# Branch A of a hybrid encoder step: weight differences on DVE, and the accumulator read ahead of the weight preparation

## The chip, the cores and the metric

The kernel runs on one core of one Trainium2 chip. A core has a matrix engine (PE, with its weight loads shown as PEld), a vector engine (DVE), an activation engine (ACT), a general engine (POOL) and a queue that starts transfers (SP). Each engine works through its own list of instructions in the order in which they stand there; an instruction that has to wait holds up everything behind it on its engine. The metric is device microseconds (us) of the whole kernel; less is better. Before the change it was 1235.42 us, the median of three runs (1234.3 to 1236.22).

## What is computed

One layer of a streaming encoder on 1024 prompt tokens and 32 sample tokens, width 1024. The part that matters here is the input projection and branch A:

```
h = rmsnorm(x);  z = h @ w_in                      # 1056 x 1024  times  1024 x 8192
qa, fa, va, ga, xb, gb, qc, gc, za, zb, zc = split(z)
f  = lb + (1-lb)*sigmoid(fa)                       # branch A: gated linear recurrence, 4 heads x 128
oa = hgrn2(silu(qa), log f, 1-f, va, state)        # chunks of 64 tokens, a 128 x 128 state per head
pa = (rmsnorm(oa) * silu(ga)) @ w_a_down
pb = (lru(conv(xb)) * silu(gb)) @ w_b_down         # branch B
pc = (attention(qc, memory) * silu(gc)) @ w_c_down # branch C
y  = x + (sigmoid(za)*pa + sigmoid(zb)*pb + sigmoid(zc)*pc) @ w_out
```

All of it is float32 in effect: each matrix product is made of three products of a high and a low part.

## The kernel before, in words

The input projection is 32 products, each of them 256 output columns by all tokens, computed with Strassen's scheme in seven steps in place of eight (`WIDE` for the first 19 products, `NARROW` for the other 13, from `A_FROM` on). The activations stand ready in seven forms (A11, A12, A22, S1 to S4, each as a high and a low half). The weights of a step are a 512 x 128 block of `w_in` (`wraw`), or a difference of blocks: T1 = B12-B11, T2 = B22-T1, T3 = B22-B12 and T4 = B21-T2. The profile names the first two `T` and the last two, which are written over a block, `wraw`. `hl` splits such a block into a high half (ACT, line 41, `whi`) and a low half (DVE, line 44, `wlo`).

One step (`slot`, L362) issues, in this order:

- the first 12 matmuls (`product`, L349); then one piece of every running chain of side work (`advance`), first the fast ones, then the others;
- the other 12 matmuls; again one piece of each chain; and then everything that a table holds for this step (`run_sched`, L293): the split of the weights used three steps later, the four differences of the next product at fixed steps (T1 at a product's step 2, counted from 0, T2 at step 3, T3 at 5, T4 one product later at 1), and the loads of the product after the next at step 6;
- at the end `post` (L305), which reads the step's accumulator out of PSUM.

In the NARROW order the accumulators are X, Y, X, V, Z, V, Z for steps 0 to 6, in two buffers of PSUM. X is copied after step 0 (ACT, L310) and after step 2 (ACT, `c11`); Y is read after step 1 (DVE, L314, `u<-Y`); V is read after step 3 (DVE, L314, `p<-V`) and after 5, Z after 4 and 6 (DVE, lines 172, 764 to 770 and 839 to 845). V in step 3 takes the buffer of Y, so it may start only when `u<-Y` has ended; Z in step 4 takes that of X.

The 13 NARROW products are, for each of four heads, `AHand1` (f and v), `AHand2` (q and g) and a pair of branch C (`Row`, `zh`), and one merge-gate pair at the end. Each head's side work hangs on them: the elementwise chains of L774 and L848, and `hgrn` (L867), the recurrence, which begins in step 4 of the C product and ends in step 3 of the next head's first one. One piece of it is a few small matmuls on PE (`pu`, `po`), then on DVE `qr` (L924), `R` (L908) and `attm` (L886), on ACT the state `S`, a sum of squares and `kt` (L888), and on POOL the inverse root `rsr` (lines 97 and 98). Every third piece PE transposes `qr` (`pot`, L933).

The differences of weights are made by `sub`, on the engine that `eng` names: DVE for the first 19 products, POOL for the other 13. They are 512-column subtractions, four for each product.

Of the kernel before, what the change touches and what calls it, by code (L numbers as in the profile page):

```python
# [32 lines left out]
def kernel(ctx: ExitStack, tc: tile.TileContext, I, O):  # L33
    nc = tc.nc
# [43 lines left out]
    def advance(lst):  # L78
        for g in list(lst):
            try:  # L80
                next(g)
            except StopIteration:
                lst.remove(g)
# [51 lines left out]
    def dbank(name):  # L135
        return psum["d"].tile([128, 2, 512], F32, tag="d", name=name)

    def rblock(name):
        return wp.tile([128, 4, 128], F32, tag="wr", bufs=W_RAW, name=name)

    def load_block(src, r0, c0):
        t = rblock("wraw")
        nc.sync.dma_start(t, src[r0:r0 + 512, c0:c0 + 128].rearrange("(k p) c -> p k c", p=128))
        return t
# [6 lines left out]
    def hl(x, eng=None):  # L151
        h = wp.tile([128, 4, 128], F32R, tag="wh", bufs=W_HL, name="whi")
        l = wp.tile([128, 4, 128], F32R, tag="wl", bufs=W_HL, name="wlo")
        split(h, l, x, eng)
        return h, l
# [51 lines left out]
    A_FROM = len(pairs)  # L207
# [12 lines left out]
    def order(p):  # L220
        return NARROW if p >= A_FROM else WIDE
# [7 lines left out]
    def at(s, fn):  # L229
        sched.setdefault(s, []).append(fn)  # L230
# [3 lines left out]
    def plan(p):  # L234
        c1, c2, _ = pairs[p]
        pre = p < NPRE
        b = pos[p, 1 if pre else 0]
        R = {}

        def loads():  # L240
            R["B11"] = load_block(w_in, 0, c1)
            R["B12"] = load_block(w_in, 0, c2)
            R["B22"] = load_block(w_in, 512, c2)
            R["B21"] = load_block(w_in, 512, c1)

        eng = nc.gpsimd if p >= A_FROM else nc.vector

        def sub(out, x, y):
            eng.tensor_tensor(out, x, y, op=OP.subtract)

        def t1():
            R["T1"] = rblock("T1")
            sub(R["T1"], R["B12"], R["B11"])

        def t2():
            R["T2"] = rblock("T2")
            sub(R["T2"], R["B22"], R["T1"])

        def t3():
            sub(R["B12"], R["B22"], R["B12"])  # L260

        def t4():
            sub(R["B21"], R["B21"], R["T2"])

        def prep(k, name):
            if (p, k) in pos:
                e = pos[p, k]

                def go():
                    wts[e] = hl(R[name])  # L270

                at(e - 3, go)

        def pl():
            plt[p] = T1("p1l")
            nc.sync.dma_start(plt[p][:, :HF], p1d[p])

        at(b - 8, loads)
        at(b - 5, t1)
        at(b - 4, t2)  # L280
        at(b - 2, t3)
        R_NAME = {"T3": "B12", "T4": "B21"}
        for k, (_, name, _) in enumerate(order(p)):
            if name == "T4":
                at(b - 1 if pre else b + 1, t4)
            prep(k, R_NAME.get(name, name))
        if pre:
            at(max(b - 4, -1), pl)

    for p in range(NP):  # L290
        plan(p)

    def run_sched(s):  # L293
        for fn in sched.pop(s, []):
            fn()

    def v2(t):
        return t[:, :HF].rearrange("p (a n) -> p a n", a=2)
# [6 lines left out]
    def post(p, k, h):  # L305
        v = cur[order(p)[k][2]][:, :, :QF]

        def copy(name):
            cur[name] = H(name)
            nc.scalar.activation(v2(cur[name]), v, AF.Copy)  # L310

        def plus(name, tag, x):
            y = H(tag)
            nc.vector.tensor_tensor(v2(y), v, v2(cur[x]), op=OP.add)  # L314
            cur[name] = y

        if p >= A_FROM:
            if k == 0:
                copy("p1")
            elif k == 1:  # L320
                plus("u2", "u2", "p1")
            elif k == 2:
                h.c11(v, None)
            elif k == 3:
                plus("u4", "p1", "u2")
            elif k == 4:
                h.c22(v, cur["u4"])
            elif k == 5:
                h.c12(v, cur["u2"])
            else:  # L330
                h.c21(v, cur["u2"])
            return
        pre = p < NPRE
        if k == 0:
            copy("p1")
        elif k == 1:
            plus("p5", "p5", "p1") if pre else copy("p5")
        elif k == 2:
            plus("u2", "u2", "p1") if pre else copy("u2")
        elif k == 3:  # L340
            h.c11(v, cur["p1"])
        elif k == 4:
            h.c22(v, cur["p5"])
        elif k == 5:
            h.c12(v, cur["u2"])
        else:
            h.c21(v, cur["p1"] if pre else None)

    def product(ps, w, name, new, after=lambda q: None):  # L349
        wh, wl = w  # L350
        fh, fl = FORM[name]
        kw = {} if new else {"skip_group_check": True}
        for q in range(2):
            qs = slice(q * QF, (q + 1) * QF)
            o = ps[:, q, :QF]
            for i in range(4):
                nc.tensor.matmul(o, wh[:, i, :], fh[:, i, qs], start=bool(new) and i == 0, stop=False, **kw)  # L357
                nc.tensor.matmul(o, wh[:, i, :], fl[:, i, qs], start=False, stop=False, **kw)  # L358
                nc.tensor.matmul(o, wl[:, i, :], fh[:, i, qs], start=False, stop=(i == 3), **kw)  # L359
            after(q)  # L360

    def slot(e):  # L362
        p, k = ex[e]
        if "h" not in cur or cur["h"][0] != p:
            cur["h"] = (p, pairs[p][2]())
            if p < NPRE:
                cur["p1"] = plt.pop(p)
        form_, _, name = order(p)[k]
        new = (p, name) not in opened
        if new:  # L370
            opened.add((p, name))
            cur[name] = dbank(name)

        def after(q):
            advance(fast)
            advance(chains)
            if q == 1:
                run_sched(e)

        product(cur[name], wts.pop(e), form_, new, after)  # L380
        post(p, k, cur["h"][1])


    fb = fstack.enter_context(tc.tile_pool(name="forms_b", bufs=1, reuse_waits="tile"))
# [132 lines left out]
    def T1(name, dt=F32):  # L517
        return cpool.tile([128, NT + 6], dt, tag="t", bufs=P_T, name=name)

    def H(name, bufs=1):  # L520
        return cpool.tile([128, HF], F32, tag=name, bufs=bufs, name=name)
# [497 lines left out]
    for e in range(NE):  # L1019
        if ex[e] == (A_FROM, 0):  # L1020
            open_psum(4, 2)
        slot(e)
# [459 lines left out]
```

## Time and profile before

| | |
|---|---|
| median of three runs | 1235.42 us (1234.3 to 1236.22) |
| profiled execution, its own time | 1238.35 us |
| its span | 1236.4 us |
| PE, PEld busy | 93%, 90% |
| DVE, ACT, POOL busy | 59%, 45%, 20% |
| differences of weights on DVE / on POOL | 76 / 52 instructions |
| mean TensorE clock granted | 0.967 of full speed |

Busy time is a share of the span. What a stage's limit is stands in the waits of that stage: the idle time of an engine before an instruction, and which instruction of which engine ended it. A matmul of the projection lasts 0.28 us but the next one starts 0.12 us after it, so PE is full when matmuls start 0.12 us apart.

### The profile page before, as it was taken

The page shows a single profiled execution, that of the slowest core. Times are in us where ns is not written, and L with a number is a line of the kernel's source. Part 1 is how long each engine was busy: PE and PEld are TensorE (multiplying, and loading weights), DVE is VectorE, ACT ScalarE, POOL GpSimd, SP SyncE. Part 2 cuts the span into 40 slices and gives each one's busy share as a digit, 9 for nine tenths or more (in the row PEclk, how much of TensorE's full clock was granted, in tenths as well). Part 3 has the DMA queues.
Part 4 walks back from the last instruction along what each step waited for, and adds up shares of the span by engine and source line. Part 5 has one row for each costly group of instructions (what it writes and reads, how often), then busy time and mean ns, then how long its engine had stood idle before and what let it go on. Part 6 is the DMA issues. An engine that isn't in the chain of part 4 may idle for free. (4 is left out here: it accounts for less than half of the span.)

```text
span 1236.4 us, 21526 instructions
## 1 busy us (share of the span) xinstructions
PE 1145.9 (93%) x8350; PEld 1109.9 (90%) x8350; DVE 734.4 (59%) x1332; ACT 562.2 (45%) x1131; POOL 243.9 (20%) x382
## 2 busy tenths in 40 slices
PE   5677899999999999999999999998799999999998
PEld 5667899999999999899898998997699989899997
DVE  4445456776686686675565565654545567687222
ACT  4433346666657657563354343633433343443111
POOL 3540000000000001232333323330000004364111
PEclk8878899999999999999999999998999989899999
DMA  6125313213213313221312203116745245591221
GB/s 206 54 80 166 110 49 105 90 59 100 94 59 95 98 64 104 79 73 52 86 44 65 80 33 105 36 64 234 245 136 168 83 146 172 183 314 49 103 90 39
DMA packets 141705, 130.11 MB, mean 105 GB/s; under 512 B 10904, under 2 KB 122180, under 8 KB 141604
## 3 DMA queue, kind: packets, MB, share of 16 engines
q1 hardware_dynamic: 141604, 128.75, 33.0%
q8 instruction: 65, 1.06, 0.4%
q14 instruction: 36, 0.29, 0.1%
HBM read 93.93 MB, written 34.79 MB: 104 GB/s over the span
## 5 line engine op out<-in xcount | busy, mean ns | idle before, releaser
L44 DVE TENSOR_TENSOR wlo<-wraw,whi 128x512 fp32r<-128x512 f32 x208 | 155.0, 750 | 132.3 <-ACT whi L41 131.0
L61 PE MATMUL psdn<-ph,whi 128*128 128x384 f32 (+1 forms) x384 | 128.3, 334 | 7.7 <-ACT ph L41 5.8
L41 ACT ACTIVATE whi<-wraw 128x512 fp32r<-128x512 f32 x208 | 126.3, 620 | 17.4 <-PE psmem L1005 6.7
L61 PE MATMUL psdn<-pl,whi 128*128 128x384 f32 (+1 forms) x384 | 126.4, 329 | 0.1
L61 PE MATMUL psdn<-ph,wlo 128*128 128x384 f32 (+1 forms) x384 | 126.2, 329 | 0.2 <-DVE wlo L44 0.2
L61 PEld LDWEIGHTS psdn<-ph,whi 128*128 128x128 f32 x384 | 74.1, 193 | 10.6 <-ACT ph L41 6.5
L357 PE MATMUL V<-S1h,whi 128*128 128x264 f32 x256 | 75.0, 293 | 8.3 <-DVE u L314 7.5
L357 PE MATMUL X<-A11h,whi 128*128 128x264 f32 x256 | 76.8, 300 | 4.1 <-ACT pv L463 2.6
L44 DVE TENSOR_TENSOR wlo<-T,whi 128x512 fp32r<-128x512 f32 x64 | 44.3, 692 | 58.2 <-ACT whi L41 58.2
L359 PE MATMUL X<-A11h,wlo 128*128 128x264 f32 x256 | 75.6, 295 | 0.0
L358 PE MATMUL X<-A11l,whi 128*128 128x264 f32 x256 | 75.5, 295 | 0.0
L61 PEld LDWEIGHTS psdn<-pl,whi 128*128 128x128 f32 x384 | 73.9, 192 | 1.0 <-DVE pl L44 0.7
L61 PEld LDWEIGHTS psdn<-ph,wlo 128*128 128x128 f32 x384 | 73.6, 192 | 0.9 <-DVE wlo L44 0.9
L357 PE MATMUL V<-S4h,whi 128*128 128x264 f32 x256 | 73.7, 288 | 0.0
L359 PE MATMUL V<-S1h,wlo 128*128 128x264 f32 x256 | 73.3, 286 | 0.0
L358 PE MATMUL V<-S1l,whi 128*128 128x264 f32 x256 | 73.1, 286 | 0.0
L359 PE MATMUL V<-S4h,wlo 128*128 128x264 f32 x256 | 72.8, 285 | 0.0
L358 PE MATMUL V<-S4l,whi 128*128 128x264 f32 x256 | 72.7, 284 | 0.0
L61 PE MATMUL psout<-woh,mhi 128*128 128x384 f32 (+3 forms) x216 | 68.9, 319 | 0.1
L61 PE MATMUL psout<-woh,mlo 128*128 128x384 f32 (+3 forms) x216 | 68.7, 318 | 0.2 <-DVE mlo L44 0.2
L61 PE MATMUL psout<-wol,mhi 128*128 128x384 f32 (+3 forms) x216 | 68.7, 318 | 0.0
L174 ACT ACTIVATE zh<-zh 128x528 f32<-128x528 f32 x36 | 23.3, 646 | 95.7 <-DVE zh L172 56.3
(365 smaller groups left out, 3819.9 us busy)
## 6 DMA issues: line engine op xcount, KB each, us to landing
wraw<-in_w_in SPq DMA_DIRECT2D x134, 256.0 KB, 3.5
pbd<-sgb SPq DMA_DIRECT2D x8, 528.0 KB, 2.6
zda<-zh SPq DMA_DIRECT2D x16, 264.0 KB, 2.6
zdc<-zh SPq DMA_DIRECT2D x16, 264.0 KB, 2.8
wraw<-in_w_b_down SPq DMA_DIRECT2D x16, 256.0 KB, 4.5
xf<-in_x_prompt SPq DMA_DIRECT2D x8, 512.0 KB, 3.9
wraw<-in_w_out SPq DMA_DIRECT2D x16, 256.0 KB, 4.4
out<-xf SPq DMA_DIRECT2D x8, 512.0 KB
```

What stands on the lines that cost most here:

```text
L41: nc.scalar.activation(out, in_, AF.Copy)
L44: (eng or nc.vector).tensor_tensor(out, a, hi.bitcast(F32), op=OP.subtract)
L61: nc.tensor.matmul(ps, a, b, start=st, stop=sp)
L174: nc.scalar.activation(t, t, self.act)
L357: nc.tensor.matmul(o, wh[:, i, :], fh[:, i, qs], start=bool(new) and i == 0, stop=False, **kw)
L358: nc.tensor.matmul(o, wh[:, i, :], fl[:, i, qs], start=False, stop=False, **kw)
L359: nc.tensor.matmul(o, wl[:, i, :], fh[:, i, qs], start=False, stop=(i == 3), **kw)
```

## The change

For the 13 NARROW products the differences of weights are made on DVE, and `run_sched` comes after `post` in place of before it. The first 19 products keep their order. Lines behind L376 stand two lines further down in the changed kernel.

```diff
-        eng = nc.gpsimd if p >= A_FROM else nc.vector
+        eng = nc.vector
...
         def after(q):
             advance(fast)
             advance(chains)
-            if q == 1:
+            if q == 1 and p < A_FROM:
                 run_sched(e)
 
         product(cur[name], wts.pop(e), form_, new, after)
         post(p, k, cur["h"][1])
+        if p >= A_FROM:
+            run_sched(e)
```

PE's list is the same instruction for instruction; POOL's has 52 instructions less, DVE's 52 more (128 differences of weights where 76 stood). Three places of DVE's list show the move. The first is in steps 1 and 2 of the second head's first product, where the recurrence of the first head comes to its end (`sga` is its gated output). Before:

```order
L906 TENSOR_TENSOR R<-pu,S_6170 128x128
L938 SCALAR_TENSOR_TENSOR sga<-pot,VT,sga 128x384
L44 TENSOR_TENSOR wlo<-wraw,whi 128x512
L314 TENSOR_TENSOR u_6945<-Y,p_6870 128x528
L924 TENSOR_SCALAR qr<-po,rsr 32x128
L44 TENSOR_TENSOR wlo<-wraw,whi 128x512
L938 SCALAR_TENSOR_TENSOR sga<-pot,VT,sga 128x288
```

Now:

```order
L908 TENSOR_TENSOR R<-pu,S_6170 128x128
L940 SCALAR_TENSOR_TENSOR sga<-pot,VT,sga 128x384
L314 TENSOR_TENSOR u_6940<-Y,p_6866 128x528
L44 TENSOR_TENSOR wlo<-wraw,whi 128x512
L249 TENSOR_TENSOR wraw<-wraw,T_6580 128x512
L926 TENSOR_SCALAR qr<-po,rsr 32x128
L44 TENSOR_TENSOR wlo<-wraw,whi 128x512
L249 TENSOR_TENSOR T_6978<-wraw 128x512
L940 SCALAR_TENSOR_TENSOR sga<-pot,VT,sga 128x288
```

The read of Y has passed a weight's low half, and two differences (T4 and T1) stand among the rows that were POOL's.

The second place is inside the recurrence, at step 5 of a C product (`zh<-V` is the read of that step's accumulator). Before:

```order
L886 COPY_PREDICATED attm_856<-bd,pu 128x128
L44 TENSOR_TENSOR wlo<-T_7528,whi 128x512
L172 TENSOR_TENSOR zh<-V,u_7460 128x528
L924 TENSOR_SCALAR qr<-po,rsr 128x128
L908 SCALAR_TENSOR_TENSOR R<-R,dec,pu 128x128
L886 COPY_PREDICATED attm_855<-bd,pu 128x128
```

Now:

```order
L888 COPY_PREDICATED attm_856<-bd,pu 128x128
L172 TENSOR_TENSOR zh<-V,u_7455 128x528
L249 TENSOR_TENSOR wraw<-wraw 128x512
L44 TENSOR_TENSOR wlo<-T_7530,whi 128x512
L926 TENSOR_SCALAR qr<-po,rsr 128x128
L910 SCALAR_TENSOR_TENSOR R<-R,dec,pu 128x128
L888 COPY_PREDICATED attm_855<-bd,pu 128x128
```

The read and a difference (T3) now stand between `attm` and the low half.

The third place is steps 0 to 4 of the same C product, where the chain of L848 (`q`, `eb`, `sga`) and the first piece of the recurrence (`attm`) meet. Before:

```order
L44 TENSOR_TENSOR wlo<-T_7242,whi 128x512
L856 TENSOR_TENSOR q<-q,qr 128x528 x2
L44 TENSOR_TENSOR wlo<-wraw,whi 128x512
L314 TENSOR_TENSOR u_7460<-Y,p_7426 128x528
L859 TENSOR_TENSOR eb<-eb,q 128x528 x2
L44 TENSOR_TENSOR wlo<-wraw,whi 128x512
L864 TENSOR_TENSOR sga<-sga,ga 128x528 x2
L44 TENSOR_TENSOR wlo<-wraw,whi 128x512
L314 TENSOR_TENSOR p_7530<-V,u_7460 128x528
L886 COPY_PREDICATED attm_855<-bd,pu 128x128
```

Now:

```order
L44 TENSOR_TENSOR wlo<-T_7244,whi 128x512
L858 TENSOR_TENSOR q<-q,qr 128x528 x2
L314 TENSOR_TENSOR u_7455<-Y,p_7422 128x528
L44 TENSOR_TENSOR wlo<-wraw,whi 128x512
L249 TENSOR_TENSOR wraw<-wraw,T_7284 128x512
L861 TENSOR_TENSOR eb<-eb,q 128x528 x2
L44 TENSOR_TENSOR wlo<-wraw,whi 128x512
L249 TENSOR_TENSOR T_7495<-wraw 128x512
L866 TENSOR_TENSOR sga<-sga,ga 128x528 x2
L314 TENSOR_TENSOR p_7524<-V,u_7455 128x528
L44 TENSOR_TENSOR wlo<-wraw,whi 128x512
L249 TENSOR_TENSOR T_7530<-wraw,T_7495 128x512
```

Three differences (T4, T1 and T2) have come in between the first low half and `attm`, which is the next row.

## Rows read from the trace of the kernel before

**Rows 1.** Page, part 1: engine, busy us, share of the span, instructions.
```profile
PE   1145.9 (93%) x8350; PEld 1109.9 (90%) x8350; DVE 734.4 (59%) x1332; ACT 562.2 (45%) x1131; POOL 243.9 (20%) x382
```
**Rows 2.** Stretches from:to: length, busy of each engine, clock, DMA share, GB/s.
```profile
515.00:845.00 330.00, 315.34 (x2541) 306.05 (x2541) 196.97 (x364) 148.81 (x326) 106.08 (x147) 0.99 0.23 70
...
680.50:684.00 3.50, 3.50 (x16) 3.11 (x17) 1.00 (x3) 0.00 (x0) 2.09 (x3) 0.54 0.00 0
```
**Rows 3.** Waits of PE, 515 to 845: us in total, times, longest.
```profile
PE V L357 <- DVE u L314: 7.5, 9, 1.8
PE pot L933 <- DVE qr L924: 4.0, 4, 1.0
PE pu L895 <- ACT kt L888: 1.6, 4, 0.4
PE Z L357 <- ACT f L760: 0.9, 1, 0.9
PE Z L357 <- DVE ga L839: 0.5, 1, 0.5
```
**Rows 4.** Timeline of PE, 601 to 603: start, us, instruction, [idle before, releaser].
```profile
600.66 0.28 PE L358 MATMUL X<-A12l,whi 128*128 128x264 f32 x1
600.78 0.28 PE L359 MATMUL X<-A12h,wlo 128*128 128x264 f32 x1
602.85 0.36 PE L357 MATMUL V<-S1h,whi 128*128 128x264 f32 x1 [1.79 <-DVE u L314]
```
**Rows 5.** Timeline of DVE, the same place.
```profile
598.71 3.38 DVE L44 TENSOR_TENSOR wlo<-wraw,whi 128x512 fp32r<-128x512 f32 x1
602.01 0.69 DVE L314 TENSOR_TENSOR u<-Y,p 128x528 f32<-128x528 f32 x1
```
**Rows 6.** Timeline of POOL, the same place.
```profile
599.02 1.28 POOL L249 TENSOR_TENSOR wraw<-wraw,T 128x512 f32<-128x512 f32 x1
600.26 1.27 POOL L249 TENSOR_TENSOR T<-wraw 128x512 f32<-128x512 f32 x1
```
**Rows 7.** Line 249: count, ns min/median/max, first and last start.
```profile
L249 DVE TENSOR_TENSOR T<-wraw x19: 679/683/687, 50.7 to 478.2; 128x512 f32<-128x512 f32 x19
...
L249 POOL TENSOR_TENSOR T<-wraw x13: 1267/1293/1770, 491.4 to 794.4; 128x512 f32<-128x512 f32 x13
```
**Rows 8.** Groups of DVE, 520 to 845: count, busy, mean ns, idle before, releaser.
```profile
L44 DVE TENSOR_TENSOR wlo<-wraw,whi 128x512 fp32r<-128x512 f32 x64 | 53.8, 840 | 40.5 <-ACT whi L41 40.5
...
L856 DVE TENSOR_TENSOR q<-q,qr 128x528 f32<-128x528 f32 x8 | 9.7, 1248 | 0.0
```
**Rows 9.** The first group on DVE, 150 to 480, where POOL makes no differences.
```profile
L44 DVE TENSOR_TENSOR wlo<-wraw,whi 128x512 fp32r<-128x512 f32 x74 | 50.9, 688 | 77.2 <-ACT whi L41 75.9 <-DMA wraw<-in_w_in 1.3
```
**Rows 10.** Timeline of DVE, recurrence, steps 5 and 6 of a C product.
```profile
660.01 0.69 DVE L44 TENSOR_TENSOR wlo<-T,whi 128x512 fp32r<-128x512 f32 x1 [1.22 <-ACT whi L41]
660.62 0.70 DVE L172 TENSOR_TENSOR zh<-V,u 128x528 f32<-128x528 f32 x1
661.24 0.34 DVE L924 TENSOR_SCALAR qr<-po,rsr 128x128 f32<-128x128 f32 x1
...
665.59 0.69 DVE L44 TENSOR_TENSOR wlo<-wraw,whi 128x512 fp32r<-128x512 f32 x1 [1.22 <-ACT whi L41]
```
**Rows 11.** Timeline of ACT, first NARROW product, step 2.
```profile
524.49 0.61 ACT L41 ACTIVATE whi<-wraw 128x512 fp32r<-128x512 f32 x1
```
**Rows 12.** Timeline of POOL: an inverse root beside the low half at 665.59.
```profile
665.24 0.55 POOL L98 TENSOR_TENSOR rsr<-rsv,neghalf 128x1 f32<-128x1 f32 x1
```
**Rows 13.** Timeline of DVE, steps 1 to 4 of a C product.
```profile
641.45 0.69 DVE L44 TENSOR_TENSOR wlo<-T,whi 128x512 fp32r<-128x512 f32 x1 [3.98 <-ACT whi L41]
642.06 2.41 DVE L856 TENSOR_TENSOR q<-q,qr 128x528 f32<-128x528 f32 x2
...
650.74 0.30 DVE L886 COPY_PREDICATED attm<-bd,pu 128x128 f32<-128x128 uint32 x1 [0.76 <-PE pu L881]
```
**Rows 14.** Timeline of PE, the first product behind the projection.
```profile
852.75 0.76 PE L1003 MATMUL psmem<-whi,mh 128*128 128x512 f32 x1 [4.15 <-DVE zh L172]
```

## The prediction

> **What bounds the kernel now.** I began with the page's first part: PE is busy 93% of the span, its weight loads 90% [rows 1]. So the time of the kernel is PE's list of instructions plus the moments in which PE stands still, and the change leaves that list as it is. What it can give or take is the standing still. The view of stretches shows where the change acts: in the 330 us from 515 to 845, the NARROW products, PE is busy 315.3 us, DVE 197.0 and POOL 106.1 [rows 2]. About 15 us of PE are open there, DVE has some 130 us free.
>
> Then the waits of PE in that stretch [rows 3]. All are short and end with a DVE or an ACT instruction: 7.5 us in nine waits of V for `u<-Y`, 4.0 us in four waits of `pot` for `qr`, 1.6 us in four waits of `pu` for `kt`, 0.9 us once for `f<-X`, 0.5 us once for `ga`; 14.5 us together.
>
> Then the timelines at the longest, a pattern that stands three times, once for each of the heads 1 to 3. PE issues its last matmul for X at 600.78 and the first for V at 602.85 [rows 4]; it waited for `u<-Y`, which ran from 602.01 to 602.70, though Y had long been complete [rows 5]. In front of `u` on DVE stood one low half that took 3.38 us [rows 5]. POOL was making two differences then, 1.28 and 1.27 us [rows 6]. Alone a low half takes 688 ns on average [rows 9]; 3.38 less 0.69 is 2.69, about the two differences of POOL. So a difference on POOL does not run beside DVE for nothing: it holds up a DVE subtraction with both inputs in SBUF. Over the stretch, low halves of raw blocks average 840 ns against 688 and the eight `q` products 1248 ns [rows 8, 9].
>
> **What the change takes away and adds, term by term.**
>
> *The differences.* 52 leave POOL (1.27 us at the least, 1.29 median) and come to DVE, where one takes 683 ns [rows 7]: 52 x 0.683 = 35.5 us more for DVE. It gets back the stretching: 64 x (840 - 688) = 9.7 us, and 8 x (1248 - 710) = 4.3 us, with 710 as 688 scaled from 512 to 528 columns [rows 8, 9]. So DVE grows by 35.5 - 14.0 = 21.5 us, from 197 to about 218 of 330. On average that is hidden in DVE's free time; where it comes at a bad moment stands below.
>
> *The read first.* `u<-Y` now stands in front of its step's low half and difference. At the place of rows 5 it can start when Y is complete, before PE has ended the 24 matmuls for X (24 x 0.12 = 2.9 us, from the starts in rows 4). For all nine waits of V the same holds: no reader of Y is behind a low half any more, and nothing of POOL stretches the chain pieces ahead of it. I take the whole 7.5 us [rows 3].
>
> *kt and qr.* In the recurrence DVE stands idle 1.22 us before the low half, for ACT's high half, with the read of the accumulator (0.70 us) and then `qr` queued behind [rows 10]. Now the read and, in step 5, the difference T3 fill that idle time (0.62 + 0.62 = 1.24, by the distance of starts in rows 10), and `qr`, `R` and `attm` follow the low half at once, 0.6 us earlier. That covers all of the 0.4 us waits for `kt` (1.6 us), and 0.6 of each 1.0 us wait for `qr`, where the same rows recur at 665.59 [rows 10]: 4 x 0.6 = 2.4 us.
>
> *f and ga.* `f<-X` stood behind a high half of 0.61 us on ACT [rows 11] and now precedes it: 0.6 of 0.9 us. The wait for `ga` follows the same pattern as V's: 0.5 us [rows 3].
>
> *Refilling.* A wait costs more than its idle time, since matmuls overlap: from 600.78 to 602.85 are 2.07 us where 0.12 would stand, so 1.95 us are lost, of which the row counts 1.79 as idle [rows 4]. 0.16 us for each of the 14 waits that go (nine, four and one): 2.2 us.
>
> *The clock.* After the second of the long waits PE is granted 0.54 of its clock for 3.5 us, most of it at the lower level of 1.2 GHz [rows 2]; it had stood still 1.8 us before. Without that wait I expect 2.4 GHz throughout: 3.5 x 0.46 = 1.6 us.
>
> Sum of gains: 7.5 + 1.6 + 2.4 + 0.6 + 0.5 + 2.2 + 1.6 = 16.4 us.
>
> *What is late next.* The tightest place is a C product's steps 1 to 4, where DVE has hardly any idle time. Before, 11 instructions ran from 641.45 to `attm` at 650.74, with 0.76 us idle at the end and 1.1 us of stretching in the two `q` (2.41 less 0.62 and 0.71) [rows 13]. Now it is 15, and the first starts some 0.6 us later because its high half on ACT stands behind the copy of X: 15 x 0.62 + 0.6 = 9.9 us, so `attm` comes at about 651.35, 0.6 us later. PE asks for `kt`, 0.6 us after `attm` begins, only after its next twelve matmuls (1.4 us), so about 0.2 us is left. I have no row for this order. The bounds are nothing, and all three differences before `attm` in each of four passes in full, 4 x 3 x 0.683 = 8.2 us. I take 0.5 us a pass, 2.0 us, near the end that my count gives.
>
> *Loads and the queue.* The loads at a product's step 6 now stand behind that step's store on SP, up to some 5 us later; they are used nine steps of 2.9 us further on, or three for T1, so I count nothing. If T1's block came too late, DVE would now wait for it where POOL did, with the low halves queued behind.
>
> *Behind the projection* the next product waits 4.15 us for the last read of Z [rows 14]; that read passes one low half, and the mem loads come after their stores. I count the two as equal.
>
> One rule of the skill speaks against moving work to DVE next to what is left on POOL. POOL keeps 36 inverse roots (four heads, nine pieces); one runs from 665.24 for 0.55 us [rows 12], and the low half beside it, from 665.59, takes 0.69 us, not stretched [rows 10]. The Trainium skill, SBUF — State Buffer, section Who interferes with whom, says that a DVE instruction with two SBUF inputs contends with a POOL instruction that reads SBUF, and that the later one waits for the other's whole length. By that rule the 36 roots could take up to 36 x 0.55 = 20 us out of DVE or be held by it, and the gain would shrink to a few us; by the row, a root of one column costs DVE nothing, and that decides. The same rule does fit the 3.38 us of rows 5.
>
> **The forecast.** 16.4 - 2.0 = 14.4 us. The profiled execution took 1238.35 us itself, so it would take 1224; it lies 2.9 us above the median of the three runs, 1235.42, and from that the forecast is 1221.0.
>
> **Rivals.**
>
> *The reads help, the recurrence loses.* V's waits go, with their refilling and the clock (7.5 + 9 x 0.16 + 1.6 = 10.5), but the differences between `attm` and the low half delay `qr` and `kt`, whose 5.6 us double. For: one of the four differences of a product falls into the recurrence's steps 5 and one into its step 1, and each piece is a round of PE, DVE, ACT and POOL. Against: the idle 1.22 us of rows 10. 10.5 - 5.6 = 4.9 us: 1230.5.
>
> *No change.* What follows the projection is bound by transfers that don't move, and the wait of rows 14 grows by what was gained. For: 4.15 us are lost there already. Against: every load waits for a buffer that a step frees, and DMA is busy 23% of the stretch [rows 2], so the loads come earlier with the steps. 1235.
>
> *Slower: DVE becomes the bound.* A low half that comes late makes PE wait at the first matmul that reads it. It decides once DVE's work for a step is more than PE's 2.9 us and the three steps between a weight's preparation and its use are eaten up. If none of the 21.5 us net found cover, 21.5 - 16.4 = 5.1 us more: 1240.5. For: DVE is in order, and a step of the C product already holds two low halves, two long products and a read. Against: 130 us free, 40.5 us of them straight before low halves [rows 2, 8].
>
> **How the numbers follow.** Forecast 0.71, with its own range 1213 to 1228 (all gains, with the rest of `qr`'s 1.6 us and a little more; or 8.2 us of new waits). Reads alone 0.15, no change 0.08, slower 0.06. To hold 8 in 10 the range takes in the reads alone: 1213 to 1231. A measurement can tell 0.2%, 2.5 us, from no change. Faster: 0.71 + 0.15 = 0.86. Within 0.2%: 0.08. Slower: 0.06.
>
> **What would show it.** Right: the wait of V for `u` gone from PE's waits, `kt` too, `qr` at 0.4 us each or less; low halves at 0.69 us on average; no 1.2 GHz within the NARROW products; PE's time there shorter by 13 to 16 us and the rest moved forward as it is. Wrong: a new wait of `pu` or `po` for `attm` or `kt` in a C product's step 4; a wait of a matmul for `wlo`; a DVE difference that waits for a load; or a wait longer than 4.15 us behind the projection. The forecast fails if DVE's new 35 us show up in PE's waits.

## The result

The changed kernel takes 1220.4 us (median of 4 runs, 1218.7 to 1222.2) against 1235.8 for the kernel before in the same comparison (4 runs, 1234.3 to 1236.2): a ratio of 0.9886, with a 95% interval of 0.987 to 0.9902. Its profiled execution took 1218.74 us, its span is 1216.6.

### The profile after

The page's first part, same columns as [rows 1]:

```profile
PE 1134.9 (93%) x8350; PEld 1101.0 (90%) x8350; DVE 743.3 (61%) x1384; ACT 561.8 (46%) x1131; POOL 171.9 (14%) x330
```

The 52 differences moved from POOL's count (382 to 330) to DVE's (1332 to 1384). POOL lost 72.0 us. DVE gained only 8.9, though one of these instructions takes 0.683 us there, 35.5 us for all: the part on the prediction comes back to it.

Where the span became shorter is read from the marks that both programs share: the first matmul of X in the first NARROW product and the first matmul of the last Z step. Between them lie 332.76 us before and 318.99 after. The stretch between the marks, of before and then of after (length, busy time of PE, weight loads, DVE, ACT, POOL, clock, DMA share, GB/s):

```profile
512.76:845.52 332.76, 318.10 (x2561) 308.81 (x2562) 199.21 (x366) 149.38 (x326) 107.72 (x148) 0.99 0.24 72
```
```profile
507.70:826.69 318.99, 314.94 (x2561) 307.19 (x2562) 207.90 (x415) 149.36 (x326) 41.21 (x99) 1.00 0.24 75
```

That is 13.8 us in the stage of the change. Behind it stand 390.8 us before and 389.9 after. The stage also begins 5.1 us earlier (507.70 against 512.76). Of that 4.1 us arise ahead of the fourth product, whose first matmul starts at 150.4 us before and at 146.3 after; in the other runs below that leave the program's start as it is, it lies between 146.2 and 149.8, so I don't count it to the change.

All waits of PE from 505 to 832 of the changed kernel (us in total, times, longest), to be held against [rows 3]. The wait of X for `zh` ends at the first mark, so it lies ahead of the stretch; it stood in the kernel before too, at 512.76, just ahead of the window of [rows 3].

```profile
PE pot L935 <- DVE qr L926: 1.5, 4, 0.4
PE X L357 <- ACT zh L179: 1.4, 1, 1.4
PE V L357 <- DVE p L314: 0.6, 1, 0.6
PE ptst L744 <- POOL ST L736: 0.6, 1, 0.6
PE Z L357 <- ACT f L762: 0.4, 1, 0.4
PE pu L897 <- ACT kt L890: 0.4, 1, 0.4
```

The nine waits of V for `u` are gone, `pot` waits 0.4 us where it waited 1.0, the wait for `ga` is gone. Three are new: V for `p`, 0.6 us, once, in the first head, behind the scans; a transpose of branch B (`ptst`), 0.6 us, once; and the wait for `kt`. That last one is not left over from the four of [rows 3]. Those stood at the third piece of the recurrence, once in each head, and are gone; this one stands at the first piece, in step 4 of the first head's C product. PE before, at the second head, and now:

```profile
662.82 0.38 PE L895 MATMUL pu<-v,kt 128*128 128x128 f32 x1 [0.39 <-ACT kt L888]
```
```profile
570.23 0.49 PE L897 MATMUL pu<-v,kt 128*128 128x128 f32 x2 [0.39 <-ACT kt L890]
```

At the place of [rows 4 to 6], DVE now reads:

```profile
592.65 0.62 DVE L940 SCALAR_TENSOR_TENSOR sga<-pot,VT,sga 128x384 f32<-128x384 f32 x1 [0.39 <-PE pot L935]
593.19 0.70 DVE L314 TENSOR_TENSOR u<-Y,p 128x528 f32<-128x528 f32 x1
593.80 0.68 DVE L44 TENSOR_TENSOR wlo<-wraw,whi 128x512 fp32r<-128x512 f32 x1
594.40 0.69 DVE L249 TENSOR_TENSOR wraw<-wraw,T 128x512 f32<-128x512 f32 x1
```

`u` goes ahead of its step's low half; the low half takes 0.68 us instead of 3.38, and V starts without a wait. Over the stage, the low halves of raw blocks (count, busy, mean ns, idle before, releaser), against 840 ns in [rows 8]; those of `T` average 689:

```profile
L44 DVE TENSOR_TENSOR wlo<-wraw,whi 128x512 fp32r<-128x512 f32 x66 | 45.3, 686 | 31.2 <-ACT whi L41 30.9
```

The place that I had called the tightest, steps 1 to 4 of a C product, held 12 instructions ahead of `attm` before (the third list of the change). Now it holds 15, of which the first and the last are shown here, with DVE's three differences among them:

```profile
560.42 0.69 DVE L44 TENSOR_TENSOR wlo<-T,whi 128x512 fp32r<-128x512 f32 x1 [3.89 <-ACT whi L41]
561.03 1.32 DVE L858 TENSOR_TENSOR q<-q,qr 128x528 f32<-128x528 f32 x2
...
568.38 0.68 DVE L44 TENSOR_TENSOR wlo<-wraw,whi 128x512 fp32r<-128x512 f32 x1
568.98 0.68 DVE L249 TENSOR_TENSOR T<-wraw,T 128x512 f32<-128x512 f32 x1
569.58 0.29 DVE L888 COPY_PREDICATED attm<-bd,pu 128x128 f32<-128x128 uint32 x1
```

The rows left out have no bracket of idle time either: DVE works 9.16 us through, and `attm` comes just when PE asks for it (in the first head 0.4 us late). In the other three heads the same stretch is 9.16 to 9.17 us long, without a wait of PE. The experiments come back to this place.

### The profile page after: what moved, and what is told of

Read it like the earlier page. It is cut to its first block, busy times and chain, and to the rows that moved or that the text cites. A ratio compares the mean times of both kernels' runs of the same rounds, so it can differ in the third digit from the quotient of the medians.

```text
span 1216.6 us, 21490 instructions
## 1 busy us (share of the span) xinstructions
PE 1134.9 (93%) x8350; PEld 1101.0 (90%) x8350; DVE 743.3 (61%) x1384; ACT 561.8 (46%) x1131; POOL 171.9 (14%) x330
## 5 line engine op out<-in xcount | busy, mean ns | idle before, releaser
L44 DVE TENSOR_TENSOR wlo<-wraw,whi 128x512 fp32r<-128x512 f32 x208 | 144.8, 701 | 120.9 <-ACT whi L41 120.5
```

The costliest lines, as they stand in the source:

```text
L44: (eng or nc.vector).tensor_tensor(out, a, hi.bitcast(F32), op=OP.subtract)
```

## The experiments

Theory: the gain comes from two things, the read that goes ahead of the weights' preparation and the end of the stretching that POOL causes on DVE; DVE's added work is hidden. Rivals: one half alone does it all; the cover is thin, and it is only the end of the stretching that pays for the added work. In what follows "the stage" is the stretch between the two marks above, and each ratio is to the kernel before.

### The two halves apart

Only the engine changed, the order of the kernel before:

```diff
-        eng = nc.gpsimd if p >= A_FROM else nc.vector
+        eng = nc.vector
```

> Half of the change: the differences of the 13 NARROW products on DVE, run_sched before post as it was. Before: 1235.7 us, both halves: 1220.4 us. My theory: either half alone takes away the nine waits of V for u (7.5 us idle, 1.4 refilling, 1.6 of clock), since without POOL the low half in front of u takes 0.69 us in place of 3.38; the waits of pu for kt (1.6 us) and of pot for qr (4.0 us) stay, because the read still stands behind the low half that waits for ACT. About 10 us gained: 1225 to 1227 us. Rival A, POOL's stretching is the whole cause: 1220 to 1222 us. Rival B, the order is the whole cause: 1231 us or more, with V's waits still there.

Measured: 1225.6 us, ratio 0.9924 (0.9905 to 0.9942). Then only the order, with the differences left on POOL:

> The other half: run_sched after post for the 13 NARROW products, their differences still on POOL. My theory: the reads pass the stretched low halves, so V's waits go (10.5 us with refilling and clock) and the waits for kt and qr shrink as in the full change; POOL still stretches low halves to some 840 ns on average, but nothing of PE stands right behind them. 1220 to 1222 us, the same as the full change within 2 us. Rival A, the stretching is the cause: V's waits stay at several us and the time is 1230 us or more. Rival B, the order is the whole cause: 1218 to 1221 us, below the full change, since DVE is spared 35 us.

Measured: 1220.6 us, ratio 0.9882 (0.9861 to 0.9903). PE's longest waits in the stage, of the run with DVE alone and then of the run with the order alone:

```profile
PE pot L933 <- DVE qr L924: 4.0, 4, 1.0
PE pu L895 <- ACT kt L888: 1.6, 4, 0.4
PE X L357 <- ACT zh L179: 1.4, 1, 1.4
PE Z L357 <- ACT f L760: 1.0, 1, 1.0
PE V L357 <- DVE u L314: 0.6, 1, 0.6
```
```profile
PE V L357 <- DVE u L314: 2.0, 4, 0.9
PE X L357 <- ACT zh L179: 1.4, 1, 1.4
PE V L357 <- DVE p L314: 1.1, 1, 1.1
PE Z L357 <- ACT f L762: 0.4, 1, 0.4
```

The engine alone takes V's waits for `u` from 7.5 to 0.6 and leaves `pot`, `kt` and `f` as they were. The order alone takes V's from 7.5 to 2.0 and the recurrence's waits too, all of `pot` and `kt`. So the halves do not add: either takes most of V's waits, and the order by itself gives the whole gain. This is so although POOL goes on stretching DVE in that run. Its low halves of raw blocks (same columns as above):

```profile
L44 DVE TENSOR_TENSOR wlo<-wraw,whi 128x512 fp32r<-128x512 f32 x65 | 58.7, 904 | 25.8 <-ACT whi L41 25.8
```

They average 904 ns, more than the 840 of [rows 8], and no wait of PE ends behind one any more: the reads now stand ahead of them. What the stretching still costs there are V's four waits for `u`: `u` stands behind two `q` products, which average 1250 ns in this run and 701 in the changed kernel. Moving the differences to DVE takes these 2.0 us away and brings `pot` 1.5, `kt` 0.4 and `ptst` 0.6 in their place, so that the two come out alike (stage 318.2 and 319.0 us). Theory and rival split here: what counts is the order; the engine pays only where the order is bad.

### The new order in the wide products too

> The full change, with the read ahead of run_sched in all 32 products, the 19 WIDE ones too. In the changed kernel PE still waits seven times 0.42 us for gb (the read of step 4 before step 6) and 1.44 us for the last copy of product 18. If the order is what counts: the seven waits go with 0.16 us of refilling each (4.1 us), the 1.44 us shrink by a high half of 0.6 us: 1215 to 1217 us. If the WIDE products, whose DVE is busier, have low halves that then come too late, or ACT's reads hold up the high halves: 1220 us or more, with waits for wlo or whi on PE.

The edit takes away the condition on the product, so that every step reads first:

```diff
-            if q == 1 and p < A_FROM:
-                run_sched(e)
...
-        if p >= A_FROM:
-            run_sched(e)
+        run_sched(e)
```

Measured: 1224.5 us, ratio 0.9915 (0.9897 to 0.9932), where 1215 to 1217 was expected; it is no better than the changed kernel (0.987 to 0.9902), and rather worse. The waits of PE from 137 to 506 that differ most, of this run and then of the changed kernel:

```profile
PE pr L61 <- DVE xl L44: 6.9, 7, 1.0
```
```profile
PE X L357 <- DVE gb L643: 2.9, 7, 0.4
PE pr L61 <- DVE xl L44: 2.5, 7, 0.4
```

The seven waits for `gb` go as expected, but the wait of branch B's gate product (`pr`) for `xl` grows from 0.36 to 1.0 us each, which fits weights that are prepared one read later at the end of a product. The two come out even: from the fourth product to the stage it takes 360.7 us against 361.4. No matmul of the projection waits for `wlo` or `whi` there, the sign that the expectation had named for a loss. The loss lies ahead of the fourth product, whose first matmul starts at 152.1 us against 146.3. In all the kernels that leave that part as it is, the start lies anywhere from 146.2 to 150.4, so how much of the 5.7 us is the edit's is open. A narrower edit has the new order in step 4 alone, from the fourth product on:

```diff
+        first = p >= A_FROM or (k == 4 and p >= NPRE)
...
-            if q == 1 and p < A_FROM:
+            if q == 1 and not first:
```

> The changed kernel with its new order also at step 4 of those wide products whose weights are prepared inside the pass before (not of the first ones), where PE waits for gb (2.9 us in 7 waits). Theory: the waits go and, with 0.16 us of refilling each, 4.1 us: about 1216.5 us (1215 to 1218), if pr's wait on xl stays at the 0.35 us each (7) that it has in the changed kernel. Rival: the weights prepared at step 4 come later by the reading, and xl with them, as in the run that had the new order at every step: pr's waits grow to 1.0 each (+4.5 us), and the time is 1220 to 1222 us.

Measured: 1218.1 us, ratio 0.9867 (0.9842 to 0.9891). In its trace the waits for `gb` are gone and those for `xl` stay at 2.5 us in 7; the part from the first matmul of the fourth product to the stage takes 356.9 us, 4.5 less than in the changed kernel, where 4.1 was expected. The interval overlaps that of the changed kernel, so that the trace carries this, not the time.

### One difference back to POOL

```diff
-            sub(R["B12"], R["B22"], R["B12"])
+            (nc.gpsimd if p >= A_FROM else eng).tensor_tensor(R["B12"], R["B22"], R["B12"], op=OP.subtract)
```

> The changed kernel with one of its three differences per pass, T3, given back to POOL in the narrow products (36 of 156 differences or fewer). Theory: the waits of PE at pot on qr (4 x 0.39 us in the changed kernel, 0.1 each where only the order was changed) are DVE's T3 standing ahead of qr, and POOL has the time for it; they fall to about 0.1 each, about 1.2 us with their refilling 1.5 to 2 us go, the time is about 1218.5 us (1217.5 to 1219.5). Rival: POOL's T3 stretches DVE's instructions beside it by 1.28 us each, and some of them stand on the path as with the dummy subtractions on POOL: 1220.4 or above, up to 1225.

(A product has four differences, and T3 is 13 of the 52.)

Measured: 1219.2 us, ratio 0.988 (0.9854 to 0.9906): not to be told from the changed kernel by its time. By its trace the stage is 2.1 us shorter:

```profile
511.39:828.27 316.88, 314.10 (x2561) 307.08 (x2562) 203.21 (x403) 149.34 (x326) 56.55 (x111) 1.00 0.25 75
```

The waits of `pot` are gone from the list. But T3's own time on DVE was not what held `qr`: it lies in the idle time ahead of the low half, which starts 1.52 us after `attm` in the changed kernel (649.86 to 651.38) and with T3 on POOL (652.99 to 654.51) alike. What held `qr` was POOL's inverse root. DVE and POOL in the changed kernel, step 5 of a C product:

```profile
650.67 0.68 DVE L249 TENSOR_TENSOR wraw<-wraw 128x512 f32<-128x512 f32 x1
651.38 0.69 DVE L44 TENSOR_TENSOR wlo<-T,whi 128x512 fp32r<-128x512 f32 x1
652.51 0.35 DVE L926 TENSOR_SCALAR qr<-po,rsr 128x128 f32<-128x128 f32 x1 [0.44 <-POOL rsr L98]
650.75 0.66 POOL L97 TENSOR_SCALAR rsv<-ss 128x1 f32<-128x1 f32 x1 [1.45 <-ACT po L921]
651.49 0.99 POOL L98 TENSOR_TENSOR rsr<-rsv,neghalf 128x1 f32<-128x1 f32 x1
```

With T3 on POOL:

```profile
654.51 0.69 DVE L44 TENSOR_TENSOR wlo<-T,whi 128x512 fp32r<-128x512 f32 x1 [0.62 <-ACT whi L41]
655.12 0.34 DVE L926 TENSOR_SCALAR qr<-po,rsr 128x128 f32<-128x128 f32 x1
653.88 0.19 POOL L97 TENSOR_SCALAR rsv<-ss 128x1 f32<-128x1 f32 x1 [1.45 <-ACT po L921]
654.15 0.55 POOL L98 TENSOR_TENSOR rsr<-rsv,neghalf 128x1 f32<-128x1 f32 x1
```

POOL's two small instructions, each begun about 0.1 us behind a DVE subtraction, took 0.66 and 0.99 us in place of 0.19 and 0.55. So `qr` came 0.44 us after the queue was ready for it, and the pieces behind it were late by as much when PE asked for `pot`. Together with the edit of step 4:

> T3 back on POOL and the new order at step 4 of the wide products together. If both help, their gains add, since they lie in different stages: 1214.5 to 1216 us. If only one helps, 1216.5 to 1218.5; if neither, 1220 or above.

Measured: 1215.1 us, ratio 0.9837 (0.981 to 0.9864), the fastest of all; its interval lies below that of the changed kernel (0.987 to 0.9902). Both waits are gone, `gb` and `pot`, as in the two runs apart, and the stage takes 316.8 us and the wide part ahead of it 357.3, much as there.

### How much room DVE has left

The first test of the cover added work to POOL, not to DVE. Behind each difference (on DVE) POOL makes four subtractions of 128 columns that nobody reads:

```diff
             eng.tensor_tensor(out, x, y, op=OP.subtract)
+            for _ in range(4 if p >= A_FROM else 0):
+                nc.gpsimd.tensor_tensor(jk[0], bd, rm, op=OP.subtract)
```

> The full change, and for each of the 52 differences POOL also makes four subtractions of 128 columns from constant tiles into a tile that nothing reads, so POOL is as busy with SBUF reads as before while nothing waits for it except its own inverse roots. My theory: DVE instructions with two SBUF inputs are stretched again by some 10 to 20 us in all, but PE sees little, 1221 to 1224 us. Rival A, the stretching is what PE waited for: V's waits for u come back and the time is 1228 us or more.

Measured: 1237.3 us, ratio 1.0013 (0.9998 to 1.0029): the whole gain is gone, where I had expected 1221 to 1224. In this run many of DVE's instructions that meet one of POOL's (0.61 us on average) are stretched, mostly by 0.2 to 0.3 us, and DVE is busy 223.1 us of its stage, 15.2 more than in the changed kernel:

```profile
511.63:842.29 330.66, 319.50 (x2562) 308.24 (x2562) 223.09 (x414) 149.70 (x326) 148.75 (x283) 1.00 0.23 72
```

The stage is 11.7 us longer. Another 3.9 us lie just ahead of it, where POOL's first small subtractions already run (from 487.4) and `pr` waits 2.8 us for `xh`; 1.9 us lie behind. The run with the order alone had far worse single stretches and lost nothing. What it did not have was the differences on DVE. So the question was whether stretching is special or any more of DVE's time would do. The next kernel gives DVE three small subtractions behind each difference (0.29 us each) and POOL nothing:

```diff
             eng.tensor_tensor(out, x, y, op=OP.subtract)
+            for _ in range(3 if p >= A_FROM else 0):
+                nc.vector.tensor_tensor(jk[0], bd, rm, op=OP.subtract)
```

> The changed kernel with three more subtractions of 128 columns on DVE behind each difference of the narrow products (constant tiles in, a tile that nobody reads out), POOL left as it is. It adds about as much DVE time as the differences did (52 x 3 of some 0.2 us each, 30 to 40 us). Theory A (the amount of DVE's work decides; the run with dummy subtractions on POOL lost 17 us because DVE's time in the stage rose to 224 us): here DVE's time in the stage rises to 240 us or more, and the time is 1232 us or above. Theory B (what cost there was instructions being stretched at places that PE waits for): no instruction is stretched here, low halves keep a mean of 0.69 us, and the time is 1224 us or below; the pot waits grow from 0.4 to about 1.0 us each (4), 2.5 us, so about 1223.

Measured: 1257.1 us, ratio 1.0175 (1.0143 to 1.0206). DVE's time in the stage rose by 36.5 us and the stage by 35.3, with no instruction stretched (low halves 685 and 688 ns):

```profile
511.41:865.74 354.33, 332.03 (x2562) 321.09 (x2562) 244.36 (x561) 149.99 (x326) 38.23 (x99) 0.96 0.22 67
```

More work on DVE is enough; no stretching is needed. Its longest waits of PE (line numbers move with the edits):

```profile
PE pu L900 <- ACT kt L893: 11.9, 4, 3.0
PE V L359 <- DVE p L316: 2.4, 1, 2.4
PE X L359 <- ACT p L312: 2.0, 3, 0.7
PE ptst L747 <- POOL ST L739: 1.7, 1, 1.7
```

The wait for `kt` is at the tight place: three differences stand there, so nine small subtractions, and they come out as 3.0 us of waiting. With each of these four waits PE's clock fell to its lower level for 6.8 us, from 0.6 to 0.9 us before the wait's end on, as here with the first:

```profile
582.00:589.00 7.00, 6.12 (x29) 6.13 (x30) 3.12 (x9) 2.29 (x9) 0.76 (x2) 0.51 0.10 39
```

So PE's idle time accounts for 18.2 of the 35.3 us, and the clock for some 14: half of the 24.3 us at the lower level that lie behind those waits and of 3.4 us behind V's wait for `p`. That 36.5 us of DVE cost nearly as much is chance. Two more kernels divide the small subtractions by place. One has them only behind the three differences ahead of `attm` (T4 of one product, T1 and T2 of the next, 12 of the 52):

```diff
-            for _ in range(3 if p >= A_FROM else 0):
+            for _ in range(3 if p >= A_FROM and near else 0):
```

> The changed kernel with the three extra subtractions of 128 columns on DVE only behind those three differences of a pass that stand ahead of the recurrence's first masked copy (T4 of one product, T1 and T2 of the next, 12 of 52 differences): 36 small instructions, some 11 us of DVE. In the changed kernel DVE works 9.16 us without idle in front of that copy, in the run with the extra subtractions everywhere 12 us. Theory C (the place decides: there DVE's queue is full, and all that is added is waited for): PE's wait for kt grows to 2.7 to 3.0 us in each of the four passes, 11.5 us, and with the lower clock behind it, 3.4 us each as in the run with them everywhere, 20 to 25 us in all: 1240 to 1246 us. Theory A (the amount decides: 43 us of DVE cost 37): 11 us cost 9 to 10, 1230 us.

The other has them everywhere but there (`not near`):

> The changed kernel with the three extra subtractions on DVE behind all differences of the narrow products except the twelve that stand ahead of the recurrence's first masked copy: 120 small instructions, some 32 to 35 us of DVE. Theory C (the place decides): the waits for kt stay at 0.4 us once, no lower clock behind them; what stays of the run with them everywhere are its waits V on p 2.4, X on p 2.0, ptst 1.7 and what follows them, 5 to 14 us: 1225 to 1234 us. Theory A (the amount decides: 43 us of DVE cost 37): 32 us cost 27, 1247 us.

Measured: 1235.2 us, ratio 1.0008 (0.9994 to 1.0022), and 1236.6 us, ratio 1.0018 (1.0001 to 1.0035). The stage of the first, then of the second:

```profile
508.19:841.80 333.61, 319.81 (x2561) 311.94 (x2562) 217.77 (x451) 149.54 (x326) 41.38 (x99) 0.98 0.23 72
```
```profile
509.34:842.80 333.46, 320.80 (x2561) 309.91 (x2562) 234.70 (x526) 149.68 (x326) 38.43 (x99) 0.99 0.23 72
```

Ahead of `attm`, 9.9 us more of DVE make the stage 14.6 us longer; everywhere else, 26.8 us make it 14.5 longer. So a microsecond costs about three times as much at that place (1.5 against 0.5), but neither theory held for either run: C gave 1240 at the least and A 1230 for the first, C 1234 at the most and A 1247 for the second. The first run's price can be added up. PE there:

```profile
727.91 0.49 PE L900 MATMUL pu<-v,kt 128*128 128x128 f32 x2 [2.39 <-ACT kt L893]
```

Four such waits, 10.1 us against 0.4, are 9.7. Three of the four are followed by 3.5 us at the lower level of the clock:

```profile
574.70:578.20 3.50, 3.50 (x19) 3.50 (x18) 1.76 (x5) 1.41 (x7) 0.76 (x2) 0.51 0.20 77
651.50:655.00 3.50, 3.50 (x31) 3.50 (x32) 2.52 (x7) 1.54 (x6) 0.74 (x2) 1.00 0.20 77
728.20:731.70 3.50, 3.50 (x19) 3.50 (x19) 2.06 (x5) 1.36 (x5) 0.75 (x2) 0.52 0.22 82
806.80:810.30 3.50, 3.50 (x19) 3.50 (x18) 1.89 (x5) 1.30 (x5) 0.75 (x2) 0.51 0.20 77
```

That is 3 x 3.5 x 0.49 = 5.1 us; together 14.8, for 14.6 measured. My expectation of 20 to 25 had taken 3.4 us of lost clock for each of four waits from the run with the subtractions everywhere; here the lower level lasted half as long and came three times. In the second run the waits are many small ones: `kt` 2.4 us in 8 where 0.4 once was expected, V for `p` 2.4 with 3.4 us at the lower clock behind it, X for the copy of `p` 2.0 in 3, `ptst` 1.7. The run with POOL's small subtractions shows the same kinds (X for `p` 2.7 in 4, V for `p` 1.9, `kt` 1.9 in 6), and DVE with the same 9.16 us through ahead of `attm`. So its loss fits DVE's time lost at the other places, but that is not shown by itself. POOL's own inverse roots take as long as in the changed kernel (0.60 us on average in both); the waits of `pot`, which hang on them, grow from 1.5 to 2.3 us. How much of the rest hangs on POOL is not settled.

## Why the prediction was right

The forecast was 1221.0 us, and 1220.4 came. The mechanism is the one named: PE's standing still in the NARROW products, V's wait for `u` above all. By its terms:

- *V for `u`, 7.5 us, with refilling and the clock.* Right: none of these waits is left, and the clock is 1.00 over the stage. The cause that the prediction gave is two causes, either of which is enough for most of it: the run with the engine alone leaves 0.6 us, the run with the order alone 2.0.
- *`qr`, 2.4 of 4.0 us.* The number is right: 1.5 us stay, 0.4 at each of four places. Its reason is not. With the order alone none of the 4.0 us stays, so the new order is worth the whole 1.0 us at each place; 0.4 came back because T3 and the low half on DVE held POOL's inverse root. That the two make 0.6 is luck.
- *`kt`, 1.6 us, `f`, 0.6 of 0.9, and `ga`, 0.5.* 1.6, 0.5 and 0.5 came.
- *New waits ahead of `attm`, 2.0 us.* Mis-sized: 0.4 us once, the new wait for `kt`, is all that stands there. A new wait for `kt` in step 4 was among the prediction's signs of being wrong; it came in one head of four and is small. The 15 instructions were counted rightly, 9.3 us by 15 x 0.62 against 9.16 measured, though the 11 that the prediction gives for the kernel before are 12. Two new waits that it did not foresee, V for `p` and `ptst`, make 1.2 us more. That all three come to 1.6, near the 2.0, is luck.
- *Refilling and the clock, 3.8 us.* 3.2 came: PE's busy time between the marks fell from 318.10 to 314.94.
- *DVE's growth of 21.5 us.* Mis-sized: 8.9 us by the page, 8.7 between the marks. Two steps failed. A difference was priced at its full 0.683 us, while in a full queue the next instruction starts 0.60 us after it, so that 52 cost some 31 us and not 35.5. And what DVE gets back, 14.0 us by the prediction, was some 22: it counted low halves of raw blocks and the `q` products only, and others had been stretched as well. The four `b<-b,dm` of L815, for one, average 1458 ns before and 680 in the changed kernel, 3.1 us together; the scans average 457 and 403.
- *Counted at nothing.* The loads did not matter: no difference on DVE waits for one. The wait behind the projection shrank from 4.15 us [rows 14] to 3.16, about 1 us that the prediction had not counted.
- *The sum.* 14.4 us forecast, 13.8 measured in the stage and about 1 behind it. The range's lower end, 1213, is further down than its own reason gives: 16.4 and 1.6 us of gains make 1217.4.

The rule that the prediction weighed against a row (the Trainium skill, SBUF — State Buffer, section Who interferes with whom) would have let POOL's 36 inverse roots cost up to 20 us. The trace bears it out on one side only. POOL still makes them, and no DVE instruction of the stage is stretched, also where a low half begins 0.35 us after a root. But four of the 36 roots, one in each head, began 0.11 us behind a low half and took 0.99 us in place of 0.55, and `pot`'s waits come from that (with T3 on POOL all 36 take 0.57 us at the most, and `pot` waits no more). So a small part of the rule's price was there, 1.5 us at PE, and not 20.

Of the rivals, "the reads help, the recurrence loses" fell with `qr` and `kt` both better. "No change" fell too: what follows the projection did not grow (390.8 us before, 389.9 after). "DVE becomes the bound" did not happen, but the prediction's ground against it, 130 us of free DVE time, was the wrong one: a further 10 us, rightly placed, take the whole gain back. What the forecast rests on is its count at the one place where the queue is full. And of the change's two parts the prediction did not say which was needed: the order gives all of the gain by itself, the engine by itself about two thirds.

## What to carry to other kernels

In an in-order queue, put the instruction that frees or feeds the busiest engine ahead of the preparation for later steps, before you move work between engines: here that alone gave the whole 1.2%. Try it place by place: at every step of the wide products it gave nothing in sum, at one step 4.5 us by the trace. Room on an engine is to be counted ahead of each instruction that the bound engine waits for, in consecutive instructions, and not as free time over the stage: DVE was busy 65% and had nothing left at one place of each pass. When a helper engine's work slows a neighbour, first ask whether anybody waits for the slowed instructions; and look at the helper's own small instructions, which may be the ones that are held.

## What the runs showed of the hardware

The stretching goes both ways. In the run with the order alone, POOL's T3, which always meets a DVE instruction there, never takes less than 1.67 us (ns min/median/max, first and last start), where POOL's shortest difference takes 1.27:

```profile
L249 POOL TENSOR_TENSOR wraw<-wraw x13: 1670/1740/1757, 494.3 to 801.2; 128x512 f32<-128x512 f32 x13
```

One column of inverse roots on POOL (0.55 us) stretches nothing on DVE, but is itself held to 0.99 us when it begins 0.11 us behind a low half. 128 columns of a subtraction (0.61 us on average) stretch a DVE instruction by 0.3 us at most. Not every DVE instruction is stretched: `u<-Y`, which reads one of its inputs from PSUM, takes 693 to 702 ns in all 13 cases of the kernel before, also beside POOL's differences.

With the small subtractions ahead of `attm` alone, PE stood still 2.4 to 3.0 us at four places. Behind three of them it was granted 1.2 GHz for about 3.4 us, and 2.4 GHz throughout behind the fourth, though that wait was as long (2.38 us) as another that was followed by the lower level (2.39). With the small subtractions everywhere, all four waits of 3.0 us had 6.8 us at 1.2 GHz with them. In the kernel before, one of the three waits of 1.8 us had such a stretch behind it [rows 2]; in the changed kernel's stage there is none, and no wait there is longer than 0.7 us.
